# A decoder layer on one Trainium2 core: the first norm's squares summed row by row on TensorE, 1/rms spread by the transposing product alone, and the last chunk's norm reordered

## The chip, the cores and the metric

The kernel runs on one core of one Trainium2 chip. The core has TensorE for matrix products (PE in the profile, with its weight loads apart as PEld), VectorE (DVE), ScalarE (ACT), GpSimd (POOL) and SyncE (SP), which here only issues transfers. Each engine works off its own list of instructions in order; semaphores tie the lists together. The metric is the device time of one launch in microseconds, lower is better. The time before is 1781.81 us, the median of 3 runs (1781.71 to 1782.36).

## The reference

One layer of a hybrid decoder for 1024 prompt tokens and 8 x 8 sample tokens, 1088 columns in all, model width 1024, float32. Cut to what the change touches:

```python
def rms_norm(x, g):
    xf = x.astype(jnp.float32)
    y = xf * lax.rsqrt(jnp.mean(xf * xf, axis=-1, keepdims=True) + NORM_EPS)
    return (y * g.astype(jnp.float32)).astype(x.dtype)

sh, sc, gt = ada_mod(c, lp["w_ada_mix"], lp["b_ada_mix"])
h = rms_norm(x, lp["norm_mix"]) * (1 + sc) + sh      # first norm
P = h @ lp["w_in"]
...                                                   # RWKV-7 branch, pooling branch, merge
x = x + gt * (merged @ lp["w_out"])
sh, sc, gt = ada_mod(c, lp["w_ada_mlp"], lp["b_ada_mlp"])
h = rms_norm(x, lp["norm_mlp"]) * (1 + sc) + sh      # second norm
x = x + gt * (jnp.square(jax.nn.relu(h @ lp["w_ff1"])) @ lp["w_ff2"])
y = rms_norm(x, W["norm_final"])                      # last norm
```

## The kernel before

Activations lie with features on the 128 partitions and tokens along the free axis: eight rows `x[0..7]` of 128 x 1088. Every large product is done as three TensorE products of split operands (`hi` and `lo` parts in fp32r), so TensorE is busy nearly all the time. Its order is written by hand: `Pace` keeps a clock of estimated TensorE time, draws products from a background stream, and slips foreground work in when its due time has come (the numbers that the generators `yield`). The other engines are ordered by a scheduler that works on a simulated timeline, so the place of their instructions follows from the whole program.

Names and lines that matter here (line numbers of the profile):

- `start` (L323) is the first stage. The eight rows `x` come on SP's queue (L340), the sample columns `smp` of all rows once more as one transfer on ScalarE's queue (L331), then eight tiles `aw` of the ada weights (L353) and the first two weight tiles `wraw` (L164), again on SP's queue. A transfer waits until the one issued eight places before it, on the two queues SP and ScalarE taken together, has landed.
- Of each row ScalarE makes the squares `sq` (L343). VectorE adds the eight rows up (L347), and `stats` sums the result over the partitions: for each of nine blocks of 128 tokens one product whose stationary side is the 128 x 128 block of squares and whose moving side is a single column of ones (`one0`, nine columns in the first product to clear the bank). Each of these float32 products shows as two passes on PE, so one call of `stats` over nine blocks is 18 rows of the profile.
- `rms` (L281) takes the root (ScalarE, L286) and the reciprocal (VectorE, L287) of the 128 x 9 sums, spreads each of the nine columns to 128 x 128 in a tile `R` (VectorE, L289), and transposes those blocks on TensorE against the identity (`tr`, L155), so that every partition holds 1/rms of each token. ScalarE copies the result from PSUM to `rb` (L302).
- `ada_part` multiplies the conditioning with the `aw` tiles (L254, in the profile L148 `wc<-aw,sT`), copies the result to `asb` (L255), selects from it (`wc<-kct,asb`) and gives `am` (L263) and `g` (L268). Then the normalized, modulated rows are made: `h` (L372), `hi` (L374) and `lo` (L376) into tiles `hx`. The first product of the main stream is `mm<-hx,whi`.
- `norm2` uses the same `rms` in the middle of the kernel.
- `last` and `norm3` are the end. The last eighth of the second MLP product runs over three chunks of columns, `FCH` = 448, 384 and 256. For each chunk and each row m, VectorE adds the product to `x` (`residual`, L1406 and L1409; the sample columns of the last chunk by a further addition on GpSimd, L1411), ScalarE squares it (L1383), VectorE accumulates (L1385). After row 7 `stats` and `rms` follow, then the rows are scaled (L1396; rows 7 and 6 of the last chunk on GpSimd and ScalarE, L1393 and L1394) and stored (L1397). PSUM tiles with the tag `wc` have two buffers.

The functions in full:

Of the kernel before, what the change touches and what calls it, by code (L numbers as in the profile page):

```python
# [13 lines left out]
ALU = mybir.AluOpType  # L14
# [4 lines left out]
P = 128  # L19
D = 1024  # L20
NPR = 1024
NSEQ = 8
TS = 8
NT = NPR + NSEQ * TS
# [93 lines left out]
class K:  # L118
# [159 lines left out]
            m = len(blocks) if first and i == 0 else 1  # L278
            self.mm(po[:, i:i + m], t[:, b:b + 128], self.kc("one0")[:, :m], start=first and i == 0, stop=last and i == len(blocks) - 1)

    def rms(self, po, col, blocks, out, pool):  # L281

        nc = self.nc
        k = len(blocks)
        r = self.cp.tile([P, 16], F32, tag="rt", bufs=2, name=self.nm("rt"))[:, :k]
        nc.scalar.activation(r, po[:, col:col + k], AF.Sqrt, bias=self.eps[:, 0:1], scale=1.0 / D)  # L286
        nc.vector.reciprocal(r, r)  # L287
        R = self.row(pool, "R", 1, w=9 * 128).rearrange("p (b j) -> p b j", j=128)
        nc.vector.tensor_copy(R[:, :k, :], r.unsqueeze(2).to_broadcast([P, k, 128]))  # L289
        yield 2000  # L290
        for i in range(0, k, 4):
            m = min(4, k - i)
            ps = self.ps("wc")
            for j in range(m):
                self.tr(ps[:, j * 128:(j + 1) * 128], R[:, i + j, :], self.kc("ident"))
            for j in range(m):
                if j + 1 < m and blocks[i + j + 1] == blocks[i + j] + 128:
                    continue
                a = j
                while a > 0 and blocks[i + a - 1] == blocks[i + a] - 128:  # L300
                    a -= 1
                nc.scalar.activation(out[:, blocks[i + a]:blocks[i + j] + 128], ps[:, a * 128:(j + 1) * 128], AF.Copy)  # L302
            yield 500
# [19 lines left out]
    def start(self, st, order):  # L323

        nc, io = self.nc, self.io
        self.am = self.cp.tile([P, 24, 9], F32, name="am")
        g = self.cp.tile([P, 8, 9], F32, name="g1")
        aw = lambda: st.tile([P, 1024], F32, tag="aw", bufs=8, name=self.nm("aw"))
        asb = st.tile([P, 512], F32, name="asb")
        smp = st.tile([P, 8, 64], F32, name="smp")  # L330
        nc.scalar.dma_start(smp, io["xT"][:, :, NPR:NT].rearrange("k p n -> p k n"))  # L331
        blocks = self.blocks(0, NT)
        po = self.ps("w")
        rt = self.cp.tile([P, 16], F32, tag="rt", bufs=2, name=self.nm("rt"))
        nc.scalar.activation(rt[:, 0:1], self.eps[:, 0:1], AF.Sqrt)
        xs = []
        t = None
        for kb in range(8):
            x = self.row(st, "x", 8)
            nc.sync.dma_start(x, io["xT"][kb])  # L340
            xs.append(x)
            sq = self.row(st, "sq", 3)
            nc.scalar.activation(sq, x, AF.Square)  # L343
            if t is None:
                t = sq
            else:
                nc.vector.tensor_tensor(t, t, sq, op=ALU.add)  # L347
        ws = []

        def load(i):  # L350
            for k in range(8):
                ws.append(aw())
                nc.sync.dma_start(ws[-1], io["w_ada_mix"][k, i])  # L353

        load(0)
        back = self.stream(None, order)
        self.stats(po, t, blocks, True, True)
        rb = self.row(st, "rb", 1)
        pr, sa = slice(0, NPR), slice(NPR, NT)

        def part(i, gaps, turn):
            yield from self.ada_part("w_ada_mix", i, lambda: ws.pop(0), asb, self.am, "b_mix", (4 * i, 8 + 4 * i), gaps, turn)
            self.mod_scale(g, self.am, "norm_mix", 4 * i, 4 * i + 4)
            ks = slice(4 * i, 4 * i + 4)
            seq = lambda t: t[:, ks, 1:9].unsqueeze(3).to_broadcast([P, 4, 8, 8])
            s4 = smp[:, ks].rearrange("p k (q t) -> p k q t", t=TS)
            nc.vector.tensor_tensor(smp[:, ks], smp[:, ks], rb[:, sa].unsqueeze(1).to_broadcast([P, 4, 64]), op=ALU.mult)
            nc.vector.tensor_tensor(s4, s4, seq(g), op=ALU.mult)
            nc.vector.tensor_tensor(s4, s4, seq(self.am), op=ALU.add)
            for kb in range(4 * i, 4 * i + 4):  # L370
                x, h, hi, lo, sh = xs[kb], self.row(st, "h", 2)[:, pr], self.hh[kb], self.hl[kb], self.am[:, kb, 0:1]
                nc.vector.scalar_tensor_tensor(h, x[:, pr], g[:, kb, 0:1], rb[:, pr], op0=ALU.mult, op1=ALU.mult)  # L372

                nc.scalar.activation(hi[:, pr], h, AF.Identity, bias=sh)  # L374
                nc.scalar.activation(hi[:, sa], smp[:, kb], AF.Copy)
                nc.vector.scalar_tensor_tensor(lo[:, pr], h, sh, hi[:, pr].bitcast(F32), op0=ALU.add, op1=ALU.subtract)  # L376
                nc.vector.tensor_tensor(lo[:, sa], smp[:, kb], hi[:, sa].bitcast(F32), op=ALU.subtract)

        self.pace.run(iter(()), [part(0, (0, 3500, 0, 0), 1000), self.rms(po, 0, blocks, rb, st)])
        load(1)  # L380

        def rest():
            yield from part(1, (0, 0, 3000, 1500), 1500)
            self.done.add("h")

        self.pace.run(back, [rest()], lambda: "h" in self.done)
        return back
# [807 lines left out]
    def phase2(self):  # L1195
# [55 lines left out]
        def norm2():  # L1251
            yield lambda: "ada" in self.done
            self.mod_scale(g2, self.aq, "norm_mlp")
            rb = T()
            for i, ch in enumerate((CH[:2], CH[2:])):
                a, b = ch[0][0], ch[-1][0] + ch[-1][1]
                bl = [x for c0, n in ch for x in self.blocks(c0, n)]
                po = self.ps("wc")
                acc = T()
                for m in range(8):  # L1260
                    yield lambda: ("out", m, i) in self.done
                    t = T() if m else acc
                    nc.scalar.activation(t[:, a:b], self.xr[m][:, a:b], AF.Square)
                    if 0 < m < 7:
                        nc.vector.tensor_tensor(acc[:, a:b], acc[:, a:b], t[:, a:b], op=ALU.add)  # L1265
                    if m > 5:
                        yield 3500
                        self.stats(po, acc if m == 6 else t, bl, m == 6, m == 7)
                yield from self.rms(po, 0, bl, rb, p)
                for kb in range(8):  # L1270
                    hi, lo = fh[kb][i], fl[kb][i] = MG(i), MG(i)
                    h = T()[:, a:b]
                    x, r, sh = self.xr[kb][:, a:b], rb[:, a:b], self.aq[:, kb, 0:1]
                    if i == 0 and kb % 4 < 3:

                        nc.vector.scalar_tensor_tensor(h, x, g2[:, kb, 0:1], r, op0=ALU.mult, op1=ALU.mult)  # L1276
                        nc.scalar.activation(hi, h, AF.Identity, bias=sh)
                        nc.vector.scalar_tensor_tensor(lo, h, sh, hi.bitcast(F32), op0=ALU.add, op1=ALU.subtract)  # L1278
                    else:
                        nc.vector.tensor_tensor(h, x, r, op=ALU.mult)  # L1280
                        self.modulate(h, h, g2, self.aq, kb, a, b - a, a)
                        nc.scalar.activation(hi, h, AF.Copy)
                        (nc.gpsimd if kb % 4 == 3 else nc.vector).tensor_tensor(lo, h, hi.bitcast(F32), op=ALU.subtract)
                    yield 1000
                self.done.add(("h2", i))
# [59 lines left out]
        w = []  # L1345
# [28 lines left out]
        def norm3():  # L1374
            rb = T()
            for ci, (c0, n) in enumerate(FCH):
                bl = self.blocks(0, n)
                po = self.ps("wc")
                acc = T()
                for m in range(8):  # L1380
                    yield lambda: ("ff", m, ci) in self.done
                    t = T() if m else acc
                    nc.scalar.activation(t[:, :n], self.xr[m][:, c0:c0 + n], AF.Square)  # L1383
                    if 0 < m < 7:
                        nc.vector.tensor_tensor(acc[:, :n], acc[:, :n], t[:, :n], op=ALU.add)  # L1385
                    if m > 5:
                        yield 2500
                        self.stats(po, acc if m == 6 else t, bl, m == 6, m == 7)
                yield from self.rms(po, 0, bl, rb[:, c0:c0 + n], p)
                for m in (7, 6, 0, 1, 2, 3, 4, 5):  # L1390
                    x = self.xr[m][:, c0:c0 + n]
                    if m > 5 and ci == 2:
                        nc.gpsimd.tensor_tensor(x, x, rb[:, c0:c0 + n], op=ALU.mult)  # L1393
                        nc.scalar.activation(x, x, AF.Copy, scale=self.par("norm_final", m))  # L1394
                    else:
# [134 lines left out]
```

## Time and profile before

| | |
|---|---|
| median of 3 runs | 1781.81 us (1781.71 to 1782.36) |
| time of the profiled execution | 1781.57 us |
| its span in the profile | 1779.8 us, so 1.77 us lie outside the span |
| PE busy | 1691.3 us, 95% of the span |
| VectorE / ScalarE / GpSimd busy | 893.7 / 556.0 / 239.9 us |
| mean granted TensorE clock | 0.98 |
| first product of the main stream starts | 38.49 us |
| last product of the main stream ends | 1765.70 us |

All times in the views are microseconds from the start of the span. A row of the timeline gives the start, the time taken, the engine, the line, the operation, what it writes and reads, a count where like instructions follow each other, and in brackets how long the engine was idle before and what ended the wait. A row of the table of windows gives a stretch of time and the busy time of each engine in it, then the granted clock of TensorE (1.00 is full speed), the share of the DMA engines' time and GB/s.

### The profile page before, as it was taken

Reading aid. Unit: us, or ns where it says so; the run is one execution under the profiler, and the core shown is the slowest. Engines: PE = TensorE matmul, PEld = TensorE weight load, DVE = VectorE, ACT = ScalarE, POOL = GpSimd, SP = SyncE. Lnnn points to the kernel's source line nnn. Section 1 sums busy time; section 2 is a strip of 40 time slices with the busy share of each in tenths; the row PEclk is TensorE's granted clock in tenths of the full one; section 3 lists DMA queues with packets and bytes.
Section 4 is the critical chain, followed back from the end, with each engine's and each line's share of the span. In section 5 each row is a group of like instructions: output and inputs, shape, how many; then the busy total and the mean of one; then the engine's idle time right before and its main releaser. Section 6 shows DMA issues by size and latency. Waiting matters only on the chain.

```text
span 1779.8 us, 32440 instructions
## 1 busy us (share of the span) xinstructions
PE 1691.3 (95%) x13649; PEld 1575.6 (89%) x13649; DVE 893.7 (50%) x1574; ACT 556.0 (31%) x1104; POOL 239.9 (13%) x319
## 2 busy tenths in 40 slices
PE   5899999989998999998999899999999999999997
PEld 2889878876887798888889899999999999999997
DVE  5586575757583738254535743333333333333346
ACT  4343342344344334322324531312121222212132
POOL 0100100000000000002413511111111111111111
PEclk9999999989998999999999999999999999999998
DMA  9223314222413241848752221111111111111112
GB/s 333 102 77 139 130 47 144 74 91 79 154 46 114 84 143 50 293 169 316 285 172 78 77 72 42 47 43 48 43 42 48 46 45 42 48 42 48 42 42 101
DMA packets 80082, 179.66 MB, mean 101 GB/s; under 512 B 16480, under 2 KB 23136, under 8 KB 79936
## 3 DMA queue, kind: packets, MB, share of 16 engines
q1 hardware_dynamic: 72128, 156.66, 25.5%
q10 hardware_dynamic: 7664, 20.42, 3.3%
q8 instruction: 107, 1.75, 0.4%
q0 software_dynamic: 144, 0.51, 0.1%
q14 instruction: 39, 0.32, 0.1%
HBM read 138.71 MB, written 38.84 MB: 100 GB/s over the span
## 4 chain that ended last, share of the span: by engine, by line
PE 63%; DVE 4%; DMA 1%; ACT 1%; issue 1%; POOL 0%; DVEq 0%; ACTq 0%
PE mm L148 43%; PE w L148 17%; PE wc L148 2%; DVE wt L309 1%; DMA t<-d_th 1%; DMA hx<-in_xT 1%; DVE hx L1396 0%; DVE t L1276 0%; DVE wlo L168 0%; DVE ma L1278 0%; DVE t L1265 0%; DVE hx L1406 0%; DVE bk L591 0%; DVE bk L592 0%; ACT L307 0%
## 5 line engine op out<-in xcount | busy, mean ns | idle before, releaser
L148 PE MATMUL mm<-hx,whi 128*128 128x362 f32 (+2 forms) x2608 | 690.7, 347 | 9.1 <-DVE t L1219 6.7
L148 PEld LDWEIGHTS mm<-hx,whi 128*128 128x128 f32 x2608 | 462.9, 193 | 54.0 <-issue 30.5
L148 PE MATMUL mm<-hx,wlo 128*128 128x362 f32 (+3 forms) x1304 | 431.8, 331 | 1.8 <-DVE wlo L168 1.8
L167 ACT ACTIVATE whi<-wraw 128x512 fp32r<-128x512 f32 x246 | 155.2, 631 | 562.5 <-PE w L148 376.4
L148 PE MATMUL mm<-ma,whi 128*128 128x364 f32 (+1 forms) x1280 | 319.5, 331 | 0.0
L148 PEld LDWEIGHTS mm<-hx,wlo 128*128 128x128 f32 x1304 | 251.9, 193 | 2.5 <-DVE wlo L168 2.4
L148 PEld LDWEIGHTS mm<-ma,whi 128*128 128x128 f32 x1280 | 227.6, 190 | 6.7 <-issue 5.0
L168 DVE TENSOR_TENSOR wlo<-wraw,whi 128x512 fp32r<-128x512 f32 x157 | 114.4, 729 | 235.0 <-ACT whi L167 226.8
L148 PE MATMUL mm<-ma,wlo 128*128 128x364 f32 (+1 forms) x640 | 211.2, 330 | 0.2 <-DVE wlo L168 0.2
L168 POOL TENSOR_TENSOR wlo<-wraw,whi 128x512 fp32r<-128x512 f32 x89 | 117.9, 1325 | 657.6 <-ACT whi L167 657.6
L1406 DVE SCALAR_TENSOR_TENSOR hx<-mm,aq,hx 128x364 f32<-128x364 f32 (+4 forms) x136 | 74.7, 587 | 206.4 <-PE mm L148 206.3
L148 PE MATMUL w<-mb,whi 128*128 128x362 f32 x640 | 157.7, 328 | 0.0
L148 PEld LDWEIGHTS mm<-ma,wlo 128*128 128x128 f32 x640 | 121.3, 190 | 0.5 <-DVE wlo L168 0.5
L1300 DVE TENSOR_TENSOR ft<-ft 128x362 f32<-128x362 f32 (+1 forms) x96 | 53.0, 576 | 127.4 <-ACT ft L1299 126.8
L148 PEld LDWEIGHTS w<-mb,whi 128*128 128x128 f32 x640 | 113.0, 189 | 0.0
L148 PE MATMUL w<-mb,wlo 128*128 128x362 f32 x320 | 104.9, 328 | 2.8 <-DVE wlo L168 2.8
L148 PE MATMUL w<-hx,whi 128*128 128x362 f32 x416 | 103.5, 330 | 0.0
L148 PE MATMUL mm<-hid,whi 128*128 128x364 f32 (+4 forms) x304 | 75.3, 330 | 0.0
L148 PEld LDWEIGHTS w<-hx,whi 128*128 128x128 f32 x416 | 73.6, 191 | 0.8 <-issue 0.8
L1299 ACT ACTIVATE ft<-mm 128x364 f32<-128x364 f32 x64 | 29.3, 474 | 128.0 <-PE mm L148 127.9
L148 PE MATMUL w<-hx,wlo 128*128 128x362 f32 x208 | 67.8, 326 | 0.0
L148 PEld LDWEIGHTS w<-mb,wlo 128*128 128x128 f32 x320 | 60.6, 189 | 3.5 <-DVE wlo L168 3.4
(296 smaller groups left out, 2113.9 us busy)
## 6 DMA issues: line engine op xcount, KB each, us to landing
wraw<-in_w_ff SPq DMA_DIRECT2D x134, 256.0 KB, 2.6
wraw<-in_w_in SPq DMA_DIRECT2D x68, 256.0 KB, 2.9
hid<-in_w_ada_mlp SPq DMA_DIRECT2D x24, 512.0 KB, 5.2
d_th<-px SPq DMA_DIRECT2D x22, 544.0 KB, 3.0
wt<-d_x SPq DMA_DIRECT2D x20, 544.0 KB, 4.2
t<-d_th ACTq DMA_DIRECT2D x16, 544.0 KB, 6.2
aw<-in_w_ada_mix SPq DMA_DIRECT2D x16, 512.0 KB, 7.1
wraw<-in_w_out SPq DMA_DIRECT2D x32, 256.0 KB, 2.7
```

The lines of the kernel that those rows point to most:

```text
L148: return self.nc.tensor.matmul(out, lhsT, rhs, **kw)
L167: nc.scalar.activation(hi, raw, AF.Copy)
L168: (nc.gpsimd if n % 2 and n >= self.solo else nc.vector).tensor_tensor(lo, raw, hi.bitcast(F32), op=ALU.subtract)
L309: nc.vector.reciprocal(out[:, a:min(a + 182, n)], out[:, a:min(a + 182, n)])
L1299: nc.scalar.activation(t[:, :n], ps[:, :n], AF.Relu)
L1300: nc.vector.tensor_tensor(t[:, :n], t[:, :n], t[:, :n], op=ALU.mult)
L1406: nc.vector.scalar_tensor_tensor(x[:, c0:c0 + m], ps[:, :m], gt[:, 0:1], x[:, c0:c0 + m], op0=ALU.mult, op1=ALU.add)
```

## The change

Five edits:

1. In `start`, every row of squares goes straight into `stats` as soon as it is there, eight calls in place of one; the seven additions on VectorE go away. The buffers of `sq` stay three.
2. In `rms`, the tile `R` and the VectorE copy that fills it go away in all three norms. The transposing product reads the column of 1/rms itself, broadcast with a stride of zero.
3. The sample columns `smp` are loaded from GpSimd's queue in place of ScalarE's.
4. The due times of the first `ada_part` are (4000, 0, 0, 0) in place of (0, 3500, 0, 0), which moves all its products behind the transposes.
5. In `norm3`, for the last chunk the squares of each row go straight into `stats` (eight calls in place of two, six VectorE additions less), 1/rms is not copied out of PSUM, and all eight rows are scaled on VectorE with PSUM as an operand. For the middle chunk, rows 3 to 7 are now scaled on GpSimd and ScalarE in place of VectorE. Rows are taken in the order 0 to 7.

```diff
-    def rms(self, po, col, blocks, out, pool):
+    def rms(self, po, col, blocks, out):
...
         nc.vector.reciprocal(r, r)
-        R = self.row(pool, "R", 1, w=9 * 128).rearrange("p (b j) -> p b j", j=128)
-        nc.vector.tensor_copy(R[:, :k, :], r.unsqueeze(2).to_broadcast([P, k, 128]))
         yield 2000
...
-                self.tr(ps[:, j * 128:(j + 1) * 128], R[:, i + j, :], self.kc("ident"))
+                self.tr(ps[:, j * 128:(j + 1) * 128], r[:, i + j:i + j + 1].to_broadcast([P, 128]), self.kc("ident"))
+            if out is None:
+                self.rps = ps
+                return
...
-        nc.scalar.dma_start(smp, io["xT"][:, :, NPR:NT].rearrange("k p n -> p k n"))
+        nc.gpsimd.dma_start(smp, io["xT"][:, :, NPR:NT].rearrange("k p n -> p k n"))
...
             nc.scalar.activation(sq, x, AF.Square)
-            if t is None:
-                t = sq
-            else:
-                nc.vector.tensor_tensor(t, t, sq, op=ALU.add)
+            self.stats(po, sq, blocks, kb == 0, kb == 7)
...
-        self.stats(po, t, blocks, True, True)
...
-        self.pace.run(iter(()), [part(0, (0, 3500, 0, 0), 1000), self.rms(po, 0, blocks, rb, st)])
+        self.pace.run(iter(()), [part(0, (4000, 0, 0, 0), 1000), self.rms(po, 0, blocks, rb)])
...
-                acc = T()
+                acc = T() if ci < 2 else None
...
-                    t = T() if m else acc
+                    t = T() if m or ci == 2 else acc
                     nc.scalar.activation(t[:, :n], self.xr[m][:, c0:c0 + n], AF.Square)
+                    if ci == 2:
+                        yield 1500
+                        self.stats(po, t, bl, m == 0, m == 7)
+                        continue
...
-                yield from self.rms(po, 0, bl, rb[:, c0:c0 + n], p)
-                for m in (7, 6, 0, 1, 2, 3, 4, 5):
+                yield from self.rms(po, 0, bl, rb[:, c0:c0 + n] if ci < 2 else None)
+                for m in range(8):
                     x = self.xr[m][:, c0:c0 + n]
-                    if m > 5 and ci == 2:
+                    if ci == 2:
+                        nc.vector.scalar_tensor_tensor(x, x, self.par("norm_final", m), self.rps[:, :n], op0=ALU.mult, op1=ALU.mult)
+                    elif m > 2 and ci == 1:
                         nc.gpsimd.tensor_tensor(x, x, rb[:, c0:c0 + n], op=ALU.mult)
                         nc.scalar.activation(x, x, AF.Copy, scale=self.par("norm_final", m))
                     else:
```

How the instructions stand on an engine, in its own order. First TensorE at the beginning of the program, before (`w_176` is the bank of the sums, `wc_256` that of the ada products, `wc_266` and `wc_272` those of the transposes):

```order
L148 MATMUL w_176<-kct,sq_181 128x9
L148 MATMUL w_176<-kct,sq_181 128x1 x8
L148 MATMUL wc_256<-aw_218,sT 32x512 x2
L148 MATMUL wc_256<-aw_220,sT 32x512 x2
L155 MATMUL wc_266<-kct,R_264 128x128 x4
L155 MATMUL wc_272<-kct,R_264 128x128 x4
L148 MATMUL wc_256<-aw_222,sT 32x512 x2
```

TensorE at the same place now:

```order
L148 MATMUL w_176<-kct,sq_181 128x9
L148 MATMUL w_176<-kct,sq_181 128x1 x8
L148 MATMUL w_176<-kct,sq_194 128x1 x9
L148 MATMUL w_176<-kct,sq_207 128x1 x9
L148 MATMUL w_176<-kct,sq_220 128x1 x9
L148 MATMUL w_176<-kct,sq_233 128x1 x9
L148 MATMUL w_176<-kct,sq_246 128x1 x9
L148 MATMUL w_176<-kct,sq_259 128x1 x9
L148 MATMUL w_176<-kct,sq_272 128x1 x9
L155 MATMUL wc_316<-kct,rt_313 128x128 x4
L155 MATMUL wc_322<-kct,rt_313 128x128 x4
L155 MATMUL wc_328<-kct,rt_313 128x128
```

The nine sums of one row of squares have become 72 sums of eight rows, and all nine transposes come right behind them; the ada products, of which four stood between the sums and the transposes, now begin behind all of these.

GpSimd at the end of the program, before (the additions of the sample columns, then the two scaled rows):

```order
L1411 TENSOR_TENSOR hx_9127<-hx_9127,rs_16900 128x64
L1411 TENSOR_TENSOR hx_9129<-hx_9129,rs_16945 128x64
L1411 TENSOR_TENSOR hx_9131<-hx_9131,rs_16965 128x64
L1411 TENSOR_TENSOR hx_9133<-hx_9133,rs_16985 128x64
L1411 TENSOR_TENSOR hx_9135<-hx_9135,rs_17005 128x64
L1393 TENSOR_TENSOR hx_9135<-hx_9135,t_16512 128x256
L1393 TENSOR_TENSOR hx_9133<-hx_9133,t_16512 128x256
```

GpSimd at the same place now (`hx_9181` is row 3, `hx_9189` row 7; `t_16562` is `rb`):

```order
L1413 TENSOR_TENSOR hx_9181<-hx_9181,rs_16946 128x64
L1395 TENSOR_TENSOR hx_9181<-hx_9181,t_16562 128x384
L1395 TENSOR_TENSOR hx_9183<-hx_9183,t_16562 128x384
L1395 TENSOR_TENSOR hx_9185<-hx_9185,t_16562 128x384
L1395 TENSOR_TENSOR hx_9187<-hx_9187,t_16562 128x384
L1395 TENSOR_TENSOR hx_9189<-hx_9189,t_16562 128x384
L1413 TENSOR_TENSOR hx_9183<-hx_9183,rs_16987 128x64
L1413 TENSOR_TENSOR hx_9185<-hx_9185,rs_17008 128x64
L1413 TENSOR_TENSOR hx_9187<-hx_9187,rs_17029 128x64
L1413 TENSOR_TENSOR hx_9189<-hx_9189,rs_17046 128x64
```

Five scalings of the middle chunk now stand ahead of the additions that complete rows 4 to 7 of the last chunk, on which the squares of those rows wait. Behind the last product of the main stream TensorE had the sums of two tiles of squares; now it has those of six rows (2 to 7), with those of rows 0 and 1 between the products.

On ScalarE at the beginning, the two copies `whi` of the first weight tiles stood behind the first two copies to `rb`; they now stand ahead of the root.

More of the change, by code (lines that the diff above doesn't have):

```diff
@@ L336, in start @@
         xs = []
-        t = None
         for kb in range(8):
@@ L1268, in norm2 @@
                         self.stats(po, acc if m == 6 else t, bl, m == 6, m == 7)
-                yield from self.rms(po, 0, bl, rb, p)
+                yield from self.rms(po, 0, bl, rb)
                 for kb in range(8):
```

## The prediction

> **What bounds the kernel now.** The page first: its table of engines shows who is busy.
>
> ```profile
> PE 1691.3 (95%) x13649; PEld 1575.6 (89%) x13649; DVE 893.7 (50%) x1574; ACT 556.0 (31%) x1104; POOL 239.9 (13%) x319
> ```
>
> TensorE is the bound, and whatever delays the first product of its main stream, or keeps the end waiting behind its last, adds to the time one for one. The change touches these two places; so I read the timeline there.
>
> ```profile
> 1.97 0.54 POOL L1088 DMA_DIRECT2D kct<-in_kc  x1
> 4.68 1.11 ACT L343 ACTIVATE sq<-x 128x1088 f32<-128x1088 f32 x1 [1.51 <-DMA x<-in_xT]
> 15.34 1.11 ACT L343 ACTIVATE sq<-x 128x1088 f32<-128x1088 f32 x1 [0.29 <-DMA x<-in_xT]
> 16.81 1.11 ACT L343 ACTIVATE sq<-x 128x1088 f32<-128x1088 f32 x1 [0.36 <-DMA x<-in_xT]
> 16.84 3.76 SPq L353 DMA_DIRECT2D aw<-in_w_ada_mix  x8
> 19.41 4.00 PE L148 MATMUL w<-kct,sq 128*128 128x9 f32 x18 [19.41 <-DVE sq L347]
> 23.34 1.93 PE L148 MATMUL wc<-aw,sT 128*32 128x512 f32 x8
> 23.44 0.27 ACT L286 ACTIVATE rt<-w,eps 128x9 f32<-128x9 f32 x1 [4.22 <-PE w L148]
> 23.99 1.35 DVE L289 COPY R<-rt 128x1152 f32<-128x1152 f32 x1
> 25.40 1.12 PE L155 MATMUL wc<-kct,R 128*128 128x128 f32 x4
> 26.56 0.60 ACT L302 ACTIVATE rb<-wc 128x512 f32<-128x512 f32 x1 [2.85 <-PE wc L155]
> 28.25 4.03 PE L148 MATMUL wc<-aw,sT 128*32 128x512 f32 x24
> 32.38 0.60 ACT L255 ACTIVATE asb<-wc 128x512 f32<-128x512 f32 x1
> 34.97 2.47 DVE L372 SCALAR_TENSOR_TENSOR h<-x,g,rb 128x1024 f32<-128x1024 f32 x2
> 38.49 0.97 PE L148 MATMUL mm<-hx,whi 128*128 128x364 f32 x2
> ```
>
> The norm (sums 19.41 to 23.41, root, `R`, transposes) is done in between and is not what ends last: the ada products run to 32.28, at the pace at which `aw` arrives, and from there `asb`, selection and `g` lead to `h` at 34.97. The waits of SP's queue and the table of windows say why `aw` is late: it was issued only when `smp` had landed.
>
> ```profile
> SPq L353 <- DMA smp<-in_xT: 11.2, 1, 11.2
> kct<-in_kc POOLq DMA_DIRECT2D x1, 378.5 KB, 7.2
> 20.45:23.86 3.41, 3.41 (x18) 3.07 (x22) 0.12 (x1) 0.27 (x1) 0.00 (x0) 1.00 0.95 374
> ```
>
> **TensorE's pace at the start.** The price of the new sums hangs on this. One call of `stats` over nine blocks took 4.00 us for 18 passes, 0.222 us each. Later in the kernel the same passes take about half, and so do the transposes:
>
> ```profile
> 957.56 1.39 PE L148 MATMUL wc<-kct,t 128*128 128x1 f32 x12
> 1739.99 0.60 PE L155 MATMUL wc<-kct,R 128*128 128x128 f32 x4
> 42.37 1.07 PE L148 MATMUL wc<-aw,sT 128*32 128x512 f32 x8
> ```
>
> 1.39/12 is 0.116 us a pass; four transposes 0.60 against 1.12; eight ada passes 1.07 against 1.93. So TensorE runs at half speed in the beginning, though the clock column there reads 1.00 (I go by the durations). Is it the sums themselves that would end this, if there were more of them? In the stretch 20.45 to 23.86 above TensorE was busy for all 3.41 us, nearly all of it with sums, and the transposes at 25.40 still ran at half speed. The same shows in the middle:
>
> ```profile
> 430.86 1.09 PE L148 MATMUL w<-ra,hv 64*64 64x8 f32 x16
> 432.14 1.09 PE L148 MATMUL w<-ra,hv 64*64 64x8 f32 x16
> 430.05:433.46 3.41, 3.41 (x56) 3.10 (x51) 3.41 (x6) 1.45 (x3) 0.00 (x0) 1.00 0.42 155
> 433.46:436.88 3.42, 3.42 (x18) 2.90 (x18) 3.41 (x7) 0.67 (x2) 0.00 (x0) 0.52 0.04 10
> ```
>
> TensorE was busy throughout the first stretch, 32 of the 56 products with eight columns, and in the next one the granted clock fell to 0.52. Products of a few columns do not count as work for the clock. The sums move one column, so I take 0.222 us a pass for all of them.
>
> The Trainium skill ("TensorE: Matmul & The Clock Gate", Part 1, "What's actually happening") says the opposite for this change: the clock looks at how busy TensorE was in a free-running window of 3.4 us and goes to full after one busy window, whatever was issued. By that the sums would run at half speed for one or two windows only; the rows above speak against it for one-column products. What it would give here is the first rival below.
>
> **Edit 1, sums row by row.** Removed: seven VectorE additions, which were over by 19.4. Added: 63 products, that is 8 x 18 = 144 passes instead of 18. They need `kct` (issued 1.97, landed 7.2 later: 9.2); the first square is there by then. On TensorE nothing else stands ahead of them. 9.2 + 144 x 0.222 = 41.2 for the end of the sums, against 23.4. ScalarE's squares wait for `sq` buffers from here on, at TensorE's pace, and its `whi` copies come behind; their weights have landed long before, so they hold nothing up.
>
> **Edits 2 and 4, `R` and the order.** Root and reciprocal: as before 0.58 (23.41 to 23.99), so 41.8. `R` saves 1.35 there. Nine transposes at 0.28 are 2.5, to 44.3; reading a broadcast column is not in the trace: between nothing and twice the 2.5 more, I take nothing, since the weight load has the same 128 columns. The ada products now wait behind them for a PSUM buffer, which the second copy to `rb` frees (0.60, at about 44.6). All `aw` have landed then (8 x 512 KB from 16.8 at 374 GB/s is 28), so the 32 passes run back to back: 7.7 at half speed (1.93 x 4), 4.3 at full (1.07 x 4). These have 512 columns, and before the clock came back under them, as their weight loads show:
>
> ```profile
> 29.96 0.20 PEld L148 LDWEIGHTS wc<-aw,sT 128*32 128x32 f32 x4 [0.66 <-issue]
> 30.82 0.12 PEld L148 LDWEIGHTS wc<-aw,sT 128*32 128x32 f32 x4 [0.66 <-issue]
> ```
>
> That was 2.6 us after the run of 24 had begun; with a stretch of 3.41 that may begin anywhere it is 2.6 to 6. I take 5.9 for the whole run, to 50.5. From their end to `h` it is 2.69 as before (32.28 to 34.97): 53.2, which is 18.2 later. In the other two norms `R` lies beside main products and the transposes' place on TensorE is fixed: nothing.
>
> **Edit 3, `smp`'s queue.** The `aw` transfers are issued some 11 us sooner, a real gain for the transfers, but hidden: nobody can use `aw` before 44.6. The second set of `aw` comes sooner relative to its use, 0.3 at most. `smp` itself, there by 16.84 before, is needed only after `rb`, past 43. Behind the first `h` TensorE's order is unchanged, so the delay is carried to the end of the kernel: +17.9. Pauses will fall differently into the clock's stretches: 0.5 more, between -1.7 and +1.7 (one stretch of 3.41 at half speed).
>
> **Edit 5, the end.**
>
> ```profile
> 1764.83 0.87 PE L148 MATMUL mm<-hx,ma 128*128 128x256 f32 x6
> 1768.57 1.86 PE L148 MATMUL wc<-kct,t 128*128 128x2 f32 x8 [2.87 <-DVE t L1385]
> 1770.96 0.29 DVE L289 COPY R<-rt 128x256 f32<-128x256 f32 x1
> 1771.40 0.66 PE L155 MATMUL wc<-kct,R 128*128 128x128 f32 x2 [0.97 <-DVE R L289]
> 1772.10 0.38 ACT L302 ACTIVATE t<-wc 128x256 f32<-128x256 f32 x1 [1.37 <-PE wc L155]
> 1772.52 3.40 DVE L1396 SCALAR_TENSOR_TENSOR hx<-hx,part,t 128x256 f32<-128x256 f32 x6 [1.26 <-ACT t L302]
> L1393 POOL TENSOR_TENSOR hx<-hx,t 128x256 f32<-128x256 f32 x2 | 1.8, 930 | 4.5 <-ACT t L302 4.5
> L1385 DVE TENSOR_TENSOR t<-t,t 128x256 f32<-128x256 f32 x6 | 2.5, 417 | 1.1 <-ACT t L1383 0.9
> L168 POOL TENSOR_TENSOR wlo<-wraw,whi 128x512 fp32r<-128x512 f32 x89 | 117.9, 1325 | 657.6 <-ACT whi L167 657.6
> L1411 POOL TENSOR_TENSOR hx<-hx,rs 128x64 f32<-128x64 f32 x72 | 37.6, 522 | 175.7 <-DVE rs L1409 175.1 <-DMA wraw<-in_w_out 0.5
> 1760.07 0.49 ACT L302 ACTIVATE t<-wc 128x384 f32<-128x384 f32 x1 [0.37 <-PE wc L155]
> 1767.64 0.94 ACT L1383 ACTIVATE t<-hx 128x256 f32<-128x256 f32 x2 [0.61 <-POOL hx L1411]
> ```
>
> After TensorE's last product (1765.70) the sums came at 1768.57 to 1770.43. Now the sums of rows 0 and 1 go between the products (8 passes, 1.0 later end), VectorE loses five scalings of the middle chunk, and GpSimd gets them: 1.0 to 1.3 each (between the rows at 256 and 512 columns), five from 1760.6, to 1765.6 to 1767.1. Then four additions at 0.52, squares at 0.47, and the last sums, four passes a row: 0.46 at full speed, 0.93 at half (1.86/2). The end of the sums is 1768.7 if all is quick and 1771.9 if GpSimd and the clock are slow; I take 1770.0, 0.4 sooner. Then `R` saves 0.44 (1770.96 to 1771.40) and the copy from PSUM 0.42. Eight scalings on VectorE with GpSimd idle, at about the 0.42 of an addition of that size, are 3.4 (0.3 either way for the operand in PSUM, which no row shows), as long as the six before beside GpSimd; the last store follows as before. Sum -1.3, from -2.6 to +0.6.
>
> **The sum** against the profiled execution's 1781.57 (0.24 below the median of the runs): +17.9 + 0.5 - 1.3 = 17.1, so 1798.6 us.
>
> **The rivals.**
>
> *The sums wake the clock (TensorE goes by busy time).* Then about 23 passes at 0.222 and 121 at 0.116: 9.2 + 5.1 + 14.0 = 28.3; root 28.9; transposes and the two copies to 30.9; ada at full speed 4.3, to 35.2; `h` at 37.9, +2.9. With -0.3 and -1.3: 1782.9. For it: the later sums at 0.116. Against: the two stretches of 3.41 us above.
>
> *The sums hide under the loads, and the earlier `aw` shows (faster).* At 0.081 us a pass a call fits into the 1.47 us that one row takes to arrive (15.34 to 16.81; 18 passes); the sums would end with the last row, at 19.4, and the transfers would be the bound: `aw` landed at 28, its last products 28.5, `h` at 31.2, -3.8; with -1.3 the time is 1776.5. For it: the wait of 11.2 on SP. Against: no row has a pass under 0.116. It decides below 0.081.
>
> **How the numbers follow.** The forecast has 0.88, the first rival 0.09, the second 0.03. The forecast's bounds: at the start +14.8 (ada all at full speed -1.6, `kct` and passes a little quicker -1.4) to +21 (ada all at half speed, transposes dearer); with clock and end 1792 to 1805 if all ends meet. 1793 to 1803 leaves out the rivals (0.12) and a little of both ends. About 0.2% (3.6 us) is what a measurement of this kernel can tell from no change: the first rival lies within it, mostly (0.08); faster has 0.03, slower 0.89.
>
> **What would show it.** In the profile after: the sums `w<-kct,sq` one unbroken run of 144 passes from about 9 to 41 at 0.22 us; SP issuing `aw` from about 5; the first `h` near 53; the first `mm<-hx,whi` near 56.5; from there the same work as before, 18 later. At the end GpSimd's five scalings to about 1783, and no `R`. Wrong it is if the passes are near 0.12 us or below, or if `h` starts before 45.

## The result, and the profile after

The changed kernel takes 1797.37 us (median of 4 runs, 1794.81 to 1798.82); the kernel before, on the same chip, 1781.76 (4 runs, 1779.41 to 1782.36). The ratio is 1.0081, with a 95% interval of 1.0067 to 1.0095. It is slower, as forecast; the forecast was 1798.6, the range 1793 to 1803. The profiled execution took 1797.87 us with a span of 1796.1, so 16.3 us more than the one before.

The page's table of engines, kernel after:

```profile
PE 1717.5 (96%) x13799; PEld 1603.0 (89%) x13799; DVE 878.1 (49%) x1552; ACT 556.9 (31%) x1106; POOL 245.3 (14%) x323
```

TensorE has 150 more instructions (126 of them passes of the first sums) and is busy 26 us longer. The timeline of the start, after:

```profile
5.39 11.89 SPq L350 DMA_DIRECT2D aw<-in_w_ada_mix  x8
9.09 30.85 PE L148 MATMUL w<-kct,sq 128*128 128x9 f32 x144 [9.09 <-DMA kct<-in_kc]
13.15 1.11 ACT L343 ACTIVATE sq<-x 128x1088 f32<-128x1088 f32 x1 [2.88 <-PE w L148]
39.98 0.27 ACT L286 ACTIVATE rt<-w,eps 128x9 f32<-128x9 f32 x1 [8.02 <-PE w L148]
40.55 2.28 PE L155 MATMUL wc<-kct,rt 128*128 128x128 f32 x9 [0.61 <-DVE rt L287]
43.26 5.02 PE L148 MATMUL wc<-aw,sT 128*32 128x512 f32 x32 [0.43 <-issue]
45.21 4.89 SPq L350 DMA_DIRECT2D aw<-in_w_ada_mix  x8
50.96 2.47 DVE L368 SCALAR_TENSOR_TENSOR h<-x,g,rb 128x1024 f32<-128x1024 f32 x2
52.73 1.05 PE L148 MATMUL wc<-aw,sT 128*32 128x512 f32 x4 [1.39 <-DMA aw<-in_w_ada_mix]
55.00 0.60 PE L148 MATMUL mm<-hx,whi 128*128 128x364 f32 x2
```

The sums are one unbroken run of 144 passes: TensorE waits for nothing in it, and it is ScalarE that waits for TensorE (2.88 us ahead of a square). 30.85/144 is 0.214 us a pass. `aw` is asked for at 5.39, but nobody can use it before 43.26. The main stream starts at 55.00, 16.5 later than before. The table of windows shows the granted clock beside it:

```profile
9.10:40.00 30.90, 30.84 (x144) 1.00 0.70 261
```

The clock column (the 1.00 behind the count) says full speed, at a pace that is that of half speed: experiment 2 shows the same passes at 0.1 us with the column at 1.00 and at 0.21 with the column at 0.50. In this stretch I therefore go by the durations and not by the column.

The timeline of the end, after:

```profile
1778.11 0.49 PE L155 MATMUL wc<-kct,rt 128*128 128x128 f32 x3
1779.16 4.04 DVE L1398 SCALAR_TENSOR_TENSOR hx<-hx,part,t 128x384 f32<-128x384 f32 x3 [0.30 <-ACT t L303]
1779.21 5.83 POOL L1395 TENSOR_TENSOR hx<-hx,t 128x384 f32<-128x384 f32 x5
1784.29 0.87 PE L148 MATMUL mm<-hx,ma 128*128 128x256 f32 x6
1785.00 3.00 PE L148 MATMUL wc<-kct,t 128*128 128x1 f32 x24
1785.01 1.42 POOL L1413 TENSOR_TENSOR hx<-hx,rs 128x64 f32<-128x64 f32 x4
1788.64 0.40 PE L155 MATMUL wc<-kct,rt 128*128 128x128 f32 x2 [0.64 <-DVE rt L287]
1789.09 3.22 DVE L1393 SCALAR_TENSOR_TENSOR hx<-hx,part,wc 128x256 f32<-128x256 f32 x8 [0.59 <-PE wc L155]
```

GpSimd's five scalings end at 1785.04, four additions follow, the last sums end at 1788.0, and there is neither `R` nor a copy out of PSUM. The middle chunk's transposes, which I use as a mark, in the timelines of the kernel before and of the one without edit 1 (experiment 1):

```profile
1759.55 0.49 PE L155 MATMUL wc<-kct,R 128*128 128x128 f32 x3
```

```profile
1763.47 0.49 PE L155 MATMUL wc<-kct,rt 128*128 128x128 f32 x3
```

From there (after 1778.11, before 1759.55) to the end of the span it is 17.99 us, before 20.25: 2.26 less. What lies between start and end (the body, from the first product of the main stream to that mark) grew by 18.56 - 16.51 = 2.05. The table of windows for TensorE over the body, before and after:

```profile
38.49:1759.55 1721.06, 1665.32 (x13508) 0.98 0.28 95
55.00:1778.11 1723.11, 1664.81 (x13508) 0.98 0.28 95
```

TensorE is busy for the same time, 0.51 less, so what the body grew by is waiting, 2.56 more.

### The profile page after: what moved, and what is told of

Same layout as the page of the kernel before. It is cut to its first block, busy times and chain, and to the rows that moved or that the text cites. A ratio compares the mean times of both kernels' runs of the same rounds, so it can differ in the third digit from the quotient of the medians.

```text
span 1796.1 us, 32719 instructions
## 1 busy us (share of the span) xinstructions
PE 1717.5 (96%) x13799; PEld 1603.0 (89%) x13799; DVE 878.1 (49%) x1552; ACT 556.9 (31%) x1106; POOL 245.3 (14%) x323
## 4 chain that ended last, share of the span: by engine, by line
PE 62%; DVE 4%; ACT 1%; DMA 1%; issue 1%; POOL 0%; ACTq 0%; DVEq 0%
PE mm L148 42%; PE w L148 17%; PE wc L148 2%; DVE wt L310 1%; DMA t<-d_th 1%; DMA hx<-in_xT 1%; DVE t L1272 0%; DVE wlo L168 0%; POOL hx L1395 0%; DVE ma L1274 0%; ACT z L783 0%; DVE t L1261 0%; DVE hx L1393 0%; DVE bk L587 0%; DVE bk L588 0%
```

## The experiments

**1. Which of the five edits costs it: three kernels, each with a part of the change.** The first has the new start with the old last norm.

```diff
 # the changed kernel, but in norm3:
+    # as before the change: VectorE adds the squares of the last chunk, rb is copied
+    # out of PSUM, the rows are scaled in the old order by the old engines
```

> The changed start with the old end (edits 1 to 4, no edit 5). Theory: the row-by-row sums cost the time, and the end gives some back. Then the sums are again one run of 144 passes at 0.214 us to about 40, the first h starts near 51, and the time is that of the changed kernel plus what its end saved: 1781.8 + 16 to 18.5 = 1798 to 1800.5. Rival (the end costs too, the extra products and GpSimd's scalings eat what it saves): 1797 or less, no more than the changed kernel.

Measured: 1799.61 us, ratio 1.0098 (1.0078 to 1.0117; each ratio is against the kernel before, run beside it). As expected: the sums are again 144 passes in 30.85 us, and the first `h` starts at 50.46. The second has the old start (without `R`) and the new end.

```diff
 # the changed kernel, but in start: VectorE adds the squares, one call of stats,
-        nc.gpsimd.dma_start(smp, ...
+        nc.scalar.dma_start(smp, ...
-        ... [part(0, (4000, 0, 0, 0), 1000), ...
+        ... [part(0, (0, 3500, 0, 0), 1000), ...
```

> The old start (squares added on VectorE, one call of stats, smp on ScalarE's queue, old due times; only R is gone) with the new end (edits 2 and 5). Theory: the first h near 34.5, the last stretch from the transposes of the middle chunk to the end of the span 2.3 us shorter than before, and the time 1781.8 - 2 = 1779 to 1780.5. Rival: the end gives nothing by itself, 1781 to 1783.

Measured: 1780.59, ratio 0.9991 (0.9976 to 1.0006): a tenth of a microsecond above the expected range, and not to be told from no change. Its profile does show the shorter end: from the mark to the end of the span it is 17.89, where the kernel before takes 20.25. The third undoes edit 1 alone.

```diff
             nc.scalar.activation(sq, x, AF.Square)
-            self.stats(po, sq, blocks, kb == 0, kb == 7)
+            if t is None:
+                t = sq
+            else:
+                nc.vector.tensor_tensor(t, t, sq, op=ALU.add)
...
+        self.stats(po, t, blocks, True, True)
```

> The changed kernel with edit 1 alone undone (VectorE adds the squares up, one call of stats; due times, smp's queue, R and the end as changed). Theory: with 18 passes in place of 144 the whole loss goes. Sums 19.4 to 23.3, transposes to 26.5, then all ada products, 5 to 7 us as the clock comes back, to 32 to 34, first h at 35 to 37 (the due times of edit 4 now put the ada products behind the transposes); time 1779 to 1782. Rival (the loss is in the order of edit 4 or the queue of edit 3): still 10 us or more above 1781.8.

Measured: 1782.90, ratio 1.0001 (0.9988 to 1.0014): 0.9 above the expected range, which was set around 1781.8, but the kernel before took 1782.79 beside it. The main stream starts again about where it did before (38.49):

```profile
19.77 4.00 PE L148 MATMUL w<-kct,sq 128*128 128x9 f32 x18 [19.77 <-DVE sq L348]
38.06 0.43 PE L148 MATMUL mm<-hx,whi 128*128 128x364 f32 x1
```

So edit 1 is the whole loss, and the four others together are worth nothing that the time shows; the 2.3 us at the end are there in the profiles, but the body varies by more than that from one profile to the next.

**2. Is 0.214 us a pass the half-speed clock, and what keeps it there?** 22 wide products of bf16, of 512 columns each, run ahead of the first square; the rest is the changed kernel.

```diff
+        zz = st.tile([P, 512], BF16, name="zz")
+        nc.vector.memset(zz, 0.0)
+        zp = self.ps("mm")
+        for _ in range(22):
+            nc.tensor.matmul(zp, zz[:, :128], zz, start=True, stop=True)
```

> The changed kernel with 22 products of 512 columns (bf16, on a tile of zeros, into a bank that nobody reads) ahead of the sums. Theory (products of one column do not keep the clock up): the first sums run at 0.116 us a pass, and after one or two stretches of 3.41 us they fall back to 0.214; sums over near 36 to 38.5, 1 to 3 us gained. Rival A (the clock goes by busy time): 0.116 to the end, sums over near 26 to 27, first h near 37, time near 1784. Rival B (the pace has nothing to do with the clock, but with the transfers or the fresh squares): 0.214 from the first pass.

Measured: 1800.40 us (one run); the sums end at 38.05 and the main stream starts at 52.20, 2.8 sooner than in the changed kernel. The table of windows of TensorE (stretch, busy time and instructions, granted clock, then the transfers):

```profile
9.00:10.00 1.00, 1.00 (x10) 1.00 1.02 289
10.00:11.00 1.00, 1.00 (x10) 0.93 1.02 356
11.00:12.00 1.00, 1.00 (x6) 0.50 1.03 413
13.00:20.00 7.00, 7.00 (x35) 0.50 1.02 407
20.00:30.00 10.00, 10.00 (x48) 0.50 0.89 325
30.00:38.00 8.00, 8.00 (x38) 0.50 0.21 66
```

This is the plainest view of the mechanism. The sums begin at 8.94. There are ten passes a microsecond at full clock; within 2 us the clock is taken down, and from there it is five a microsecond at 0.50. TensorE had also been idle for 1.44 us just ahead of the sums, so the fall by itself does not tell the sums from idling. But then it is busy all the time, for 27 us, and the clock does not come back before the sums end at 38.05. The pace at 0.50 is that of the changed kernel (0.21 a pass).

Next, wide products among the sums: 16 ahead, and two after each block of each row.

```diff
+                self.mm(po[:, bi:bi + mm], sq[:, bb:bb + 128], self.kc("one0")[:, :mm], ...)
+                wide(2)
```

> The changed kernel with 16 such wide products ahead of the sums and two of them behind every block's sum (two passes), 144 in all. Theory: the wide products keep the clock up, so each block takes 2 x 0.116 + 2 x 0.216 = 0.66 us; 72 blocks 48 us, sums over near 57, and the gaps between the wide products show passes at 0.116. Rival B (the pace is not the clock's): 2 x 0.214 + 2 x 0.216 = 0.86 us a block, 62 us, over near 71.

Measured: 1806.30 us (one run). The first stretch of the table of windows, and the groups by line between 8.9 and 50 us:

```profile
9.00:20.00 11.00, 10.97 (x78) 1.00 1.02 392
L340 PE MATMUL mm<-zz 128*128 128x512 bf16 x144 | 40.9, 377 | 0.0
L148 PE MATMUL w<-kct,sq 128*128 128x1 f32 (+1 forms) x144 | 20.0, 208 | 1.6 <-DMA kct<-in_kc 1.6
```

The sums are over at 49.73, with 144 wide products in between that they did not have to wait for before: 40.7 us for 72 blocks, 0.57 a block (two passes and two wide products). The rows of one group and the other overlap (a pair of wide products that starts at 9.24 takes 0.59, and the next passes start at 9.67), so the means of 377 and 208 ns are not the pace; the 0.57 is. The clock column stays at 1.00 to the end of the sums, and the pace stays the same. So TensorE stays at full speed through the same 144 passes when other products run between them, and not when they run alone. They were over sooner than I had expected (57); why a pass costs less beside wide products was not followed up. As a remedy it costs more than it brings.

**3. Edit 3 alone undone** (`smp` back on ScalarE's queue).

```diff
-        nc.gpsimd.dma_start(smp, ...
+        nc.scalar.dma_start(smp, ...
```

> The changed kernel with edit 3 alone undone (smp on ScalarE's queue again). Theory: SP issues aw only after smp has landed, near 16.8, aw is there by about 32, and nobody uses it before 43: first h within 0.5 us of the changed kernel's 50.96, time within 2 us of 1797.4. Rival (the earlier aw is worth something even so): first h later by more than 1 us.

Measured: 1792.76 (one run), 4.6 under the median of the changed kernel, where at most 2 were expected. Its timeline:

```profile
17.05 4.11 SPq L350 DMA_DIRECT2D aw<-in_w_ada_mix  x8
43.56 4.02 PE L148 MATMUL wc<-aw,sT 128*32 128x512 f32 x32 [0.43 <-issue]
53.83 0.92 PE L148 MATMUL mm<-hx,whi 128*128 128x364 f32 x2
```

`aw` is asked for 11.7 us later, and yet the main stream starts 1.2 sooner: the earlier `aw` was hidden, as forecast. The first `h` came at 50.26, 0.7 sooner and so a little outside the expected 0.5, because the 32 ada products took 4.02 in place of 5.02: full speed came back sooner under them. One run cannot decide about the rest of the 4.6; the body differed by as much between kernels whose times are equal (below).

**4. Wide products as a remedy, and a surprise.** If half speed is the evil, then TensorE might be kept at work while VectorE adds the squares: 66 wide products ahead of the sums of the kernel without edit 1, and 14 more among the ada products.

```diff
 # the kernel without edit 1, old due times of the first ada_part
+        wide(66)                     # ahead of stats
...
+                if name == "w_ada_mix" and g == 0 and 2 * k2 + i < 7:
+                    self.wide(2)     # behind each aw tile's products
```

> A version meant to beat both: VectorE adds the squares up, smp on GpSimd's queue, old due times, no R, the new end; 66 wide products fill TensorE's idle time before the sums and 14 the waits between the ada products, so that the clock is up. Theory: sums 19.4 to 21.5, aw landed by 28, ada products over near 28.5, first h near 31 (34.97 before), time 1781.8 - 4 - 2 = 1775 to 1777. Rival (the transfers or the clock do not come sooner): first h at 34 to 35, 1779 to 1780.5.

Measured: 1802.06, ratio 1.0106 (1.0084 to 1.0129): missed by far. The sums took 2.17 us, as they should, but the main stream started at 40.50, 2.4 later than without the wide products; the ada products lost some time to the wide ones among them. Most of the loss came later: against the profile of the kernel without edit 1, the same products run 2.7 us later at 70 us and 19.3 later at 1030. So once more without those, all 66 ahead of the sums:

```diff
 # the kernel without edit 1
+        for _ in range(66):
+            nc.tensor.matmul(zp, zz[:, :128], zz, start=True, stop=True)
```

> The changed kernel without row sums (VectorE adds the squares, due times of the change kept), and 66 wide bf16 products before the sums only, none among the products with w_ada_mix. Theory: the 18 passes of the sums take 2.2 us instead of 4.0, the transposes and the first of the products with w_ada_mix gain a little too, and the first product of the main stream starts at about 35.5 (38.1 without the wide ones): 1779 to 1781. Rival (the 17 us that the last run lost after the start come from the number of instructions ahead of the body or from the wide products themselves, wherever they stand): again a stall inside the main stream and 1795 or more. If the loss came from the products among those with w_ada_mix, this kernel does not show it.

Measured: 1794.65, ratio 1.0070 (1.0052 to 1.0089); again not the theory's, and its first half failed too. TensorE stood idle for 2.84 us between the wide products and the sums, the granted clock fell to 0.50 at 20.94, the sums took 2.95, and the main stream started at 38.44, no sooner than without wide products (38.06). To tell the work of the products from their mere number, the same 66 with 8 columns in place of 512:

```diff
-            nc.tensor.matmul(zp, zz[:, :128], zz, start=True, stop=True)
+            nc.tensor.matmul(zp[:, :8], zz[:, :128], zz[:, :8], start=True, stop=True)
```

> The kernel with 66 products before the sums of VectorE's squares, each cut from 512 columns to 8: the same number of instructions, hardly any work. Theory A (the number of instructions ahead of the main stream brought the stall of 3.2 us in it and most of what the body lost): the stall near 200 us is there again, and 1790 or more. Theory B (the wide products cost by their work, such as a clock that falls back more often afterwards): no stall, 1780 to 1784, and the sums take 4.0 us again as without wide products.

Measured: 1798.92, ratio 1.0078 (1.0052 to 1.0104): the time and the stall that theory A asked for. The timeline of TensorE, of this kernel:

```profile
1.20 1.93 PE L338 MATMUL mm<-zz 128*128 128x8 bf16 x66 [1.20 <-DVE zz L335]
19.79 4.00 PE L148 MATMUL w<-kct,sq 128*128 128x9 f32 x18 [16.66 <-DVE sq L353]
198.76 0.86 PE L148 MATMUL w<-hv,iv 32*32 32x32 f32 x43
203.13 0.74 PE L148 MATMUL w<-hv,iv 32*32 32x32 f32 x20 [3.51 <-issue]
```

The 66 small products take 1.93 us at a time when TensorE has nothing to do. And yet, 200 us on, TensorE stands still for 3.51 us in the middle of a run of 63 products, where nothing that the profile shows holds it up. The kernel with 512 columns has the same stall at the same product:

```profile
198.24 0.86 PE L148 MATMUL w<-hv,iv 32*32 32x32 f32 x43
202.31 0.74 PE L148 MATMUL w<-hv,iv 32*32 32x32 f32 x20 [3.22 <-issue]
```

In the kernel with 66 and 14 wide products it comes 14 products sooner (behind 29 in place of 43), and in the kernel without wide products the run has no gap:

```profile
201.04 0.64 PE L148 MATMUL w<-hv,iv 32*32 32x32 f32 x29
204.97 1.12 PE L148 MATMUL w<-hv,iv 32*32 32x32 f32 x34 [3.29 <-issue]
```

```profile
198.97 1.17 PE L148 MATMUL w<-hv,iv 32*32 32x32 f32 x63
```

So the stall sits at a fixed place in TensorE's list, counted from its beginning: behind 1492 products in all three. What it waits for there is not shown. It is not the number alone: the changed kernel has 60 instructions more than the one with the small products and no such stall; at that place in its list stands another group of products of 32 columns, `w<-iv,hv`. Two more rows of the kernel with the small products, one of the timeline and one of the table of windows of TensorE:

```profile
725.00 0.57 PE L148 MATMUL w<-hv,iv 32*32 32x32 f32 x24 [1.55 <-issue]
202.30:209.10 6.80, 5.97 (x39) 0.50 0.14 54
```

There is a second such stall, of 1.55 us, and the granted clock falls to 0.50 during the first and stays there for 6.8 us. From 70 to 1030 us this kernel loses 16 us to the profile of the kernel without edit 1 (20 to that of the kernel before). The two stalls are 5.1 of it. The other part is the clock: in that stretch its records show 78 us at half speed, against 55 in either of those two, worth about 12 by the difference. Together that is about the 16. Why the clock falls more often, apart from the stretch at the stall, stays open.

**5. Sums row by row in another form.** Is it the place (row by row on TensorE) or the form (one column a pass) that costs? Here each row of squares, in fp32r, is moved through a 128 x 128 block of ones in three products of 364 and 362 columns. The mean square then stands on all partitions, and the transposes fall away; in their place come three roots and six reciprocals over all columns (the expectation counts eight).

```diff
-            sq = self.row(st, "sq", 3)
+            sq = self.row(st, "sq", 3, F32R)
             nc.scalar.activation(sq, x, AF.Square)
-            self.stats(po, sq, blocks, kb == 0, kb == 7)
+            for q, (c0, n) in enumerate(CH):
+                self.mm(po[q][:, :n], one, sq[:, c0:c0 + n], start=kb == 0, stop=kb == 7)
...
+        for q, (c0, n) in enumerate(CH):
+            self.rinv(po[q], n, rb[:, c0:c0 + n], 1.0 / D, 0)
...
-        ... [part(0, (4000, 0, 0, 0), 1000), self.rms(po, 0, blocks, rb)])
+        ... [part(0, (0, 0, 0, 0), 1000)])
```

> The changed kernel with its row sums in another form: each row of squares, written in fp32r, is moved through a 128x128 block of ones in three products of 364, 362 and 362 columns, 24 in all, so that the mean square stands on all 128 partitions at once and the nine transposes fall away; ScalarE takes three roots (0.56 us each by the later norms' rows) and VectorE eight reciprocals (about 1.0 us each, 7.8 in all). Theory (the loss is the form, 144 one-column passes at the half-speed clock, and not that the sums are taken row by row on TensorE): the 24 products take 0.33 us each at half speed at most, 1 us a row against 1.3 us between squares, and end by about 17.5 us; the reciprocals end by 26; the w_ada_mix products run beside the loads, whose last lands near 27; h starts near 31 and the first product of the main stream near 34 (38.1 in the run without row sums): 1776 to 1780 with the few us that the body moves from run to run. Rival (sums row by row hold TensorE and ScalarE up whatever their form): the sums end after 30, no better than 1790. Second rival (what the start gains is lost in the body, as in the last run with wide products): start near 34 and yet 1783 or more.

Measured: 1779.29 (12 runs), ratio 0.9976 (0.9963 to 0.9990): faster than the kernel before by a quarter of a per cent, and so than the changed kernel. Its timeline:

```profile
8.64 0.97 PE L148 MATMUL w<-sq,one 128*128 128x364 f32 x2 [8.64 <-ACT one L337]
16.93 1.11 ACT L346 ACTIVATE sq<-x 128x1088 fp32r<-128x1088 f32 x1 [0.25 <-DMA x<-in_xT]
18.86 0.51 PE L148 MATMUL mm<-sq,one 128*128 128x362 f32 x1
19.94 7.01 DVE L310 RECIPROCAL rb<-rb 128x182 f32<-128x182 f32 x6 [12.04 <-ACT rb L308]
27.11 1.05 PE L148 MATMUL wc<-aw,sT 128*32 128x512 f32 x4 [0.23 <-DMA aw<-in_w_ada_mix]
31.40 2.47 DVE L374 SCALAR_TENSOR_TENSOR h<-x,g,rb 128x1024 f32<-128x1024 f32 x2
35.55 0.60 PE L148 MATMUL mm<-hx,whi 128*128 128x364 f32 x2
```

Here the sums keep up with the arrival of the rows and end at 19.37, 1.3 us after the last square (18.04). They do so without a faster clock: two of them take 0.81 to 0.97 us up to the last row, where the next kernel's last rows show 0.60 with the clock up. So it was not the clock alone that made the sums long, but 144 passes in place of 24 products. The ada products now wait for their loads, so the earlier `aw` of edit 3 should count at last; no run has this form with `smp` on ScalarE's queue, so that is not shown. This is the second rival's picture, reached with other products. The main stream still begins only behind 16 products of the second half of the ada stage, 30.8 to 35.6; with those later:

```diff
-            yield from part(1, (0, 0, 3000, 1500), 1500)
+            yield from part(1, (1000, 1000, 1500, 1500), 1500)
```

> The kernel with the wide row sums and, besides, later due times for the second half of the products with w_ada_mix (1000, 1000, 1500, 1500 for 0, 0, 3000, 1500), so that the first nine products of the main stream stand ahead of them. Theory: with the wide sums the main stream starts at 35.55 only because TensorE first works through 16 products with w_ada_mix that wait for their loads (30.8 to 35.6); hx is there 33.9 at the earliest, so the first product starts near 34.0 and the end moves by up to -1.5: 1776.5 to 1780. Rival (the second half of the scale is late instead, and the main stream waits for it): 1780 to 1784.

Measured: 1777.43 (12 runs), ratio 0.9972 (0.9963 to 0.9982), the lowest of all, though not to be told from the one before it. The first product of the main stream, for which 34.0 was expected:

```profile
34.16 0.67 PE L148 MATMUL mm<-hx,whi 128*128 128x364 f32 x1 [3.99 <-ACT hx L376]
```

## Why the prediction was right, point by point

- **The pace of the sums at half speed.** 0.222 us a pass was taken, 0.214 measured; the end was to be 41.2 and was 39.94. Shown to be the clock's by the wide products ahead (from 0.1 to 0.2 us a pass within 2 us) and among the sums. The Trainium skill ("TensorE: Matmul & The Clock Gate", Part 1, "What's actually happening") would have a busy window of 3.4 us release the clock. Here the 30.85 us hold at least eight whole windows in a row that were busy with sums, and the pace stayed. The length of the window agrees with the traces: with the wide products ahead, the clock's records show one stretch at 0.50 from 10.85 to 44.99, and 34.14 is ten times 3.41. What counts as busy does not agree. The first rival (1782.9) hung on that rule and fell.
- **Root, transposes, ada.** The transposes took 2.28 (2.5), so reading a broadcast column costs nothing on top; the ada products 5.02 (5.9), as the clock came back sooner under them. `h` started at 50.96 (53.2).
- **Edit 3.** Hidden, as forecast. Wrong was the small term that the second set of `aw` would come up to 0.3 sooner relative to its use: its buffers are free only when the first ada products have run, so it is asked for at 45.21 and TensorE waits 1.39 for it at 52.73. From `h` to the main stream it is 4.04 instead of 3.52. The start was +17.9 by the sum and is +16.5.
- **Clock stretches.** +0.5 was taken, at most +1.7; the body is 2.05 longer. That is outside the bound, and the cause named was not the one: in the body the clock's records show 55 us at half speed, where the kernel before has 58, so the clock gave time back. What grew is TensorE's waiting in the body, by 2.56, a term that the prediction did not have; which waits these are was not followed up. They need not be the change's doing: the body of the kernel without edit 1 takes 1725.4 us (38.06 to 1763.47), that of the kernel before 1721.1 (38.49 to 1759.55), and in the median both take the same time. For one profile against another the bound was too narrow.
- **The end.** -1.3 was taken, -2.26 measured. The sums between the products made TensorE's last product 0.9 later (1.0 forecast), and GpSimd's scalings took 1.17 each (1.0 to 1.3). Mis-sized were its additions (0.36, not 0.52) and the last passes, at full speed: the sums end 0.99 sooner, not 0.4. From there to the end it is 1.27 less, not 0.86; the eight scalings took 3.22 (3.4).
- **The sum.** 16.51 + 2.05 - 2.26 = 16.30, forecast 17.1. The terms' errors (-1.4, +1.6, -1.0) cancel in part: that the total is off by only 0.8 is in part luck.

The second rival asked for passes under 0.081 us. One-column passes never came there, the 0.1 us at full clock being the least; with 24 wide products in place of 144 passes its time (1776.5) was nearly reached (1777.43).

## What to carry to other kernels

Before work is moved to an idle TensorE, ask how many products it makes, at which clock they will run and whether their own shape keeps the clock up: 144 one-column passes took 31 us, and 24 products of 364 or 362 columns for the same sums ran beside the loads, at half speed too. And measure the whole kernel after every such change: what stands ahead of the main stream can shift it in ways that no row at the start shows.

## What the runs showed of the hardware that I had not expected

- With only one-column products running, the granted clock fell from 1.00 to 0.50 about 2 us after they began (and 3.4 us after the last wide product), and stayed there for the 27 us of unbroken work that were left.
- 66 products of eight columns, 1.93 us of work in idle time, made the kernel 14 us slower (1.0078), with a stall of 3.5 us at a fixed place in TensorE's list 200 us on. Two stalls and more time at half speed make up about all of it; what brings them on is open.
- Three scalings of 128 x 384 on VectorE took 4.04 us beside GpSimd's five, 1.35 each. In the kernel before, eight of the same shape with GpSimd idle took 0.54 each:

```profile
1760.60 4.33 DVE L1396 SCALAR_TENSOR_TENSOR hx<-hx,part,t 128x384 f32<-128x384 f32 x8
```

So giving rows to GpSimd did not shorten VectorE's part: three scalings took nearly as long as eight. With no GpSimd beside them and one operand in PSUM, eight of 128 x 256 took 3.22, 0.40 each.
